# A decoder layer on one core: shorter rope tables, a fixed order at the change to the attention, and the modulation products split and moved

## The chip, the cores and the metric

The kernel runs on one core of a Trainium2 chip. The metric is the device time of one execution in microseconds (us). Before the change it is 984.95 us, the median of three runs (981.52 to 985.64).

## The reference, cut to what matters

One conditioned decoder layer, batch 1, 1024 tokens, width 1024, everything in float32:

```
shift, scale, gate = split(c @ w_ada + b_ada)          # "modulation", three times 1024
h    = rmsnorm(x, norm_gain) * (1 + scale) + shift
proj = h @ w_in       # stick-breaking q, k, v, z | latents c_q, c_kv | k_rot | mla_z | g_a, g_b
o_a  = stick_breaking_attention(q, k, v)               # 8 heads of 64
y_a  = (o_a * silu(z)) @ w_branch_a
o_b  = latent_attention(...)    # q and k from the latents; 32 of 96 dimensions turned by rope
y_b  = (o_b * silu(mla_z)) @ w_branch_b
x    = x + gate * ((sigmoid(g_a)*y_a + sigmoid(g_b)*y_b) @ w_out);   return rmsnorm(x, final_gain)
rope(x, pos): ang = pos * 10000 ** (-2i/32);  x1*cos - x2*sin, x1*sin + x2*cos
```

The cosines and sines are computed in the kernel: the angle in turns is reduced exactly in float32 pieces, and a polynomial gives the rest.

## The kernel before, in words

Large products run in float32r (a float32 that TensorE takes in one pass). To keep the precision each operand is split into a high part and a rest, and a product is three: high by high, high by rest, rest by high. A plain float32 product is used for small things only; the trace shows it as two records.

**The opening stage** (lines 419 to 685, pool `st`) makes h transposed (`hh`, `hl`: high part and rest, one tile for each of 8 blocks k of 128 channels) and, with it, the first products of `w_in`: for token half q = 0 and then 1, six accumulators (`accu[q]`: units 0 to 3 are the value projections of four token tiles in PSUM tags g, g, s, s, unit 4 is q of head pair 0 in tag s, unit 5 its k in tag o). Step n of the loop at L619 does the products of block k = n-1 for half 0, term by term (`by_term(k, 0, 0)`, `1`, `2`, six products of 512 columns each), and between them prepares block n: `turn` transposes x, `h_hi` (ScalarE) and `h_lo` (VectorE) apply the modulation. The modulation of a block (`wa` tiles of `w_ada`, loaded in four DMAs each) is summed mostly on VectorE (`mod_first`, `mod_acc`), but the parts listed in `WA_PE` go over TensorE as products with one column. `mod_sum(k)` issues all of these and then the column sums of VectorE's accumulator; `mod_out` adds the constants. `mod_sum` runs for k = 0, 1 and then for pairs of blocks at 2, 4, 6, each at step n = k.

`load`, `load_wa`, `load_x`, `load_w` issue all loads of this stage on SP's queue, in the order in which they stand. The order of the opening stage is written out: `pin_engines(first)` ties every instruction to the one before it on its engine (SP's queue among them), in the order of the program text. Everything after it is ordered by a planner that simulates the engines' times, except where `tc.issue_after(ins)` or `keep_in_program_order` says otherwise.

**The rope tables** (`rope_tables`, L139) run on VectorE during half 1. It is a generator: after each block k the loop at L673 lets it go on by nine of its `yield`s, and L684 lets it finish. It stands on VectorE's queue between the `h_lo` of the blocks 3 to 7.

**The change to the attention** (L691 on). The q and k of pair 0 are evacuated: half 0 from `qk0` in SBUF, half 1 from the accumulators; ScalarE copies the high part, VectorE makes the rest and two copies more for k. `store_v(1, t)` evacuates the values of half 1 (ScalarE high, VectorE rest, then a DMA to DRAM), and `load_v(0)` reads them back. Then come the filler jobs (`Job`, L276): each has a weight load of 512 KB (tile `raw`, two buffers, one of which is also `qk0`), a high copy on VectorE, a rest on VectorE (`le="v"`) or GpSimd (`le="p"`, the default), and two halves of 24 products (L299). Job 0 (z of pair 0) uses the PSUM tags t and o; job 1, a merge gate, uses g and g. The fillers are spread between the steps of the attention (`sb_pair`), so that TensorE always has something to do. `gate_sum` loads the weights of the residual gate in 512 KB pieces.

The lines that the change touches most:

```
        for n in range(1, KD):
            ...
            by_term(k, 0, 0)
            if PAIR_OF[n] == n:
                mod_sum(n)
                mod_out(n)
            turn(n, 0)
            by_term(k, 0, 1)
```

Of the kernel before, what the change touches and what calls it, by code (L numbers as in the profile page):

```python
# [10 lines left out]
F32 = mybir.dt.float32  # L11
# [4 lines left out]
ALU = mybir.AluOpType  # L16
# [3 lines left out]
P = 128  # L20
# [28 lines left out]
def hybrid_layer(ctx: ExitStack, tc: tile.TileContext, x, c, positions, w_ada, b_ada, norm_gain, w_in,  # L49
# [86 lines left out]
    cos_t = base.tile([P, NT, 16], F32, name="cos_t")  # L136
    sin_t = base.tile([P, NT, 16], F32, name="sin_t")

    def rope_tables(pool):  # L139
        eng = nc.vector  # L140
        n = [0]
        slots = pool.tile([P, 32, P], F32, name="rp", tag="wa", bufs=3)

        def new(keep):
            if keep is not None:
                return slots[:, keep]
            n[0] += 1
            return slots[:, n[0] % 26]

        def ts(i, s1, op0, s2=None, op1=None, keep=None):  # L150
            o = new(keep)
            eng.tensor_scalar(out=o, in0=i, scalar1=s1, scalar2=s2, op0=op0, **({"op1": op1} if op1 else {}))
            return o

        def tt(a, b, op, keep=None):
            o = new(keep)
            eng.tensor_tensor(out=o, in0=a, in1=b, op=op)
            return o

        def near(i, unit):  # L160
            m = 1.5 * 2.0 ** 23 * unit
            r = ts(i, m, ALU.add)
            return ts(r, m, ALU.subtract)

        import numpy as np
        inv = np.float32(ROPE_BASE) ** (-np.arange(0, DR, 2, dtype=np.float32) / np.float32(DR))
        ang = new(None)
        av = ang.rearrange("p (t f) -> p t f", f=16)
        for f in range(16):
            eng.tensor_scalar(out=av[:, :, f], in0=pos_c, scalar1=float(inv[f]), scalar2=None,  # L170
                              op0=ALU.mult)
            if f % 4 == 3:
                yield
        from fractions import Fraction
        pi = Fraction(31415926535897932384626433832795028841971693993751, 10 ** 49)
        total = None
        left = ang
        for e in (20, 9, -2, None):
            if e is None:
                part, k, scale = left, Fraction(1) / (2 * pi), 1.0  # L180
# [11 lines left out]
            whole = ts(part, scale, ALU.mult) if scale != 1.0 else part  # L192
            if e is None:
                fr = ts(whole, float(k), ALU.mult)
                total = tt(total, fr, ALU.add)
                break
            t1 = ts(whole, float(k1), ALU.mult)
            yield
            t1 = tt(t1, near(t1, 1.0), ALU.subtract)
            yield  # L200
            t2 = ts(whole, float(k2), ALU.mult)
            yield
            t3 = ts(whole, float(k3), ALU.mult)
            yield
            s = tt(t1, t2, ALU.add)
            yield
            s = tt(s, t3, ALU.add)
# [5 lines left out]
        q = ts(near(turn, 0.25), 4.0, ALU.mult, keep=26)  # L213
        th = ts(tt(turn, near(turn, 0.25), ALU.subtract), 2.0 * math.pi, ALU.mult, keep=27)
        yield
        t2 = tt(th, th, ALU.mult, keep=28)
        yield

        def poly(cs):
            r = ts(t2, cs[0], ALU.mult, cs[1], ALU.add)  # L220
            for cc in cs[2:]:
                r = ts(tt(r, t2, ALU.mult), cc, ALU.add)
            return r

        fact = math.factorial
        sn = tt(poly([-1.0 / fact(11), 1.0 / fact(9), -1.0 / fact(7), 1.0 / fact(5), -1.0 / fact(3)]), t2, ALU.mult)
        yield
        sn = tt(tt(sn, th, ALU.mult), th, ALU.add, keep=29)
        yield
        cs = tt(poly([1.0 / fact(12), -1.0 / fact(10), 1.0 / fact(8), -1.0 / fact(6), 1.0 / fact(4), -0.5]), t2,  # L230
                ALU.mult)
# [4 lines left out]
        yield  # L236
        m1 = tt(odd, q, ALU.mult)
        yield
        m0 = tt(ts(odd, -1.0, ALU.mult, 1.0, ALU.add), ts(q2, -0.5, ALU.mult, 1.0, ALU.add), ALU.mult)
        yield  # L240
        cv, sv = cos_t.rearrange("p t f -> p (t f)"), sin_t.rearrange("p t f -> p (t f)")
        eng.tensor_tensor(out=cv, in0=tt(m0, cs, ALU.mult), in1=tt(m1, sn, ALU.mult), op=ALU.subtract)
        eng.tensor_tensor(out=sv, in0=tt(m0, sn, ALU.mult), in1=tt(m1, cs, ALU.mult), op=ALU.add)

    def newton(r, v, n):
# [89 lines left out]
    def evac_q(m):  # L335
        st = pairs[m]

        def f(hf, ps):
            if hf == 0:
                st.q = [qk(f"q{m}a"), qk(f"q{m}b")]  # L340
            s = hsl(hf)
            for h in range(2):
# [5 lines left out]
    def evac_k(m):  # L348
        st = pairs[m]

        def f(hf, ps):
            if hf == 0:
# [3 lines left out]
            for h in range(2):  # L356
# [62 lines left out]
    with tc.tile_pool(name="start", bufs=1, **RW, side="right") as st:  # L419
# [58 lines left out]
        def scale_x(t, eng):  # L478
# [3 lines left out]
            else:  # L482
                (nc.vector if eng == "v" else nc.gpsimd).tensor_scalar(out=xts[t], in0=xts[t], scalar1=r, scalar2=None,
                                                                       op0=ALU.mult)

        def mod_first(k):
            accs[k] = st.tile([P, 2, 2 * P], F32, name="acc", tag="acc", bufs=2)[:, :, 0:width(k)]
            wa, c0 = was[k], col[:, R_C:R_C + 1]
# [5 lines left out]
        def mod_acc(k, a, b):  # L494
            for kk in range(a, b):
                if kk not in WA_PE.get(k, ()):
                    nc.vector.scalar_tensor_tensor(out=accs[k], in0=was[k][:, :, kk, :],
                                                   scalar=col[:, R_C + kk:R_C + kk + 1], in1=accs[k], op0=ALU.mult,
                                                   op1=ALU.add)

        def mod_sum(k):
            pm = pts["m"] = ps_tile("t")
            kks = WA_PE.get(k, ())
            nj = width(k) // P
            for n, (kk, j, s) in enumerate(itertools.product(kks, range(nj), range(2))):
                nc.tensor.matmul(out=pm[:, 2 * j + s:2 * j + s + 1], lhsT=was[k][:, s, kk, j * P:(j + 1) * P],
                                 rhs=col[:, R_C + kk:R_C + kk + 1], start=n == 0, stop=False)
            for j in range(nj):
                for s in range(2):
                    nc.tensor.matmul(out=pm[:, 2 * j + s:2 * j + s + 1], lhsT=accs[k][:, s, j * P:(j + 1) * P], rhs=ones_c,  # L510
                                     start=not kks, stop=not kks or (s == 1 and j == nj - 1))

        def mod_out(k0):
            pm = pts["m"]
# [26 lines left out]
        accu = {}  # L541

        def product(k, q, unit, term):
            if q not in accu:
# [50 lines left out]
        inverse(1)  # L595
        scale_x(2, "a")
        mod_acc(0, 2, 8)
        mod_sum(0)
        scale_x(3, "a")
        mod_out(0)  # L600
        nc.vector.tensor_copy(out=pos_f, in_=pos_i)
        split_w_hi(0)
        turn(0, 0)
        split_w_lo(0)
        h_hi(0, 0)
        load_w(3)
# [12 lines left out]
        for n in range(1, KD):  # L619
# [2 lines left out]
                op(i)  # L622
            by_term(k, 0, 0)
            if PAIR_OF[n] == n:
                mod_sum(n)
                mod_out(n)
            turn(n, 0)
            by_term(k, 0, 1)
            if n in (1, 2, 4):
                mod_first(2 if n == 1 else n + 2)  # L630
# [184 lines left out]

# [2 lines left out]
    def gate_sum():  # L818
# [4 lines left out]
            nc.sync.dma_start(out=wgs[k], in_=wada[:, k, 2 * D:3 * D])  # L823

        nc.gpsimd.memset(gsum, 0.0)
        nc.sync.dma_start(out=gsum[0:1], in_=b_ada[:, 2 * D:3 * D])
        load_g(0)
        load_g(1)
        yield
        for k in range(KD):  # L830
            cc = col[:, R_C + k:R_C + k + 1]
# [586 lines left out]
```

## Time and profile before

| What | us |
|---|---|
| median of three runs | 984.95 |
| the profiled execution's own time | 984.33 |
| its span, first to last instruction | 982.5 |
| TensorE busy (97% of the span) | 953.9 |
| VectorE busy (65%) | 641.5 |
| ScalarE busy (45%) | 440.3 |
| GpSimd busy (29%) | 289.8 |

All times below count from the start of the span. PE is TensorE, DVE VectorE, ACT ScalarE, POOL GpSimd, SPq the DMA queue of SP. The chain that ended last lies on PE for 92% of the span, on DVE for 4% and on DMA for 2%. "PEclk" in the table by stretches is the granted share of TensorE's 2.4 GHz; 0.50 is 1.2 GHz.

### The profile page before, as it was taken

Reading aid. Unit: us, or ns where it says so; the run is one execution under the profiler, and the core shown is the slowest. Engines: PE = TensorE matmul, PEld = TensorE weight load, DVE = VectorE, ACT = ScalarE, POOL = GpSimd, SP = SyncE. Lnnn points to the kernel's source line nnn. Section 1 sums busy time; section 2 is a strip of 40 time slices with the busy share of each in tenths; the row PEclk is TensorE's granted clock in tenths of the full one; section 3 lists DMA queues with packets and bytes.
Section 4 is the critical chain, followed back from the end, with each engine's and each line's share of the span. In section 5 each row is a group of like instructions: output and inputs, shape, how many; then the busy total and the mean of one; then the engine's idle time right before and its main releaser. Section 6 shows DMA issues by size and latency. Waiting matters only on the chain.

```text
span 982.5 us, 14349 instructions
## 1 busy us (share of the span) xinstructions
PE 953.9 (97%) x5132; PEld 824.2 (84%) x5132; DVE 641.5 (65%) x1319; ACT 440.3 (45%) x991; POOL 289.8 (29%) x256
## 2 busy tenths in 40 slices
PE   5999699999999999999999999999999999999997
PEld 4888588888888888888888999988899998878886
DVE  5657756568655966385654454864689997595654
ACT  5453324344524443444443432543488886342211
POOL 1010235344544444354453000621103441101222
PEclk9899899999999999999999999999999999999999
DMA  9911273223331141103212500579554332792232
GB/s 311 332 53 56 87 238 95 73 64 90 129 105 46 54 139 54 54 22 97 76 65 86 150 1 1 192 274 303 180 134 135 104 97 69 248 374 95 83 118 98
DMA packets 112712, 122.39 MB, mean 125 GB/s; under 512 B 14928, under 2 KB 81597, under 8 KB 112256
## 3 DMA queue, kind: packets, MB, share of 16 engines
q1 hardware_dynamic: 112550, 121.44, 39.3%
q8 instruction: 41, 0.67, 0.3%
q14 instruction: 31, 0.25, 0.1%
q10 hardware_dynamic: 90, 0.02, 0.0%
HBM read 86.80 MB, written 34.64 MB: 124 GB/s over the span
## 4 chain that ended last, share of the span: by engine, by line
PE 92%; DVE 4%; DMA 2%; issue 1%; ACT 0%; DVEq 0%; SPq 0%
PE ps_g L299 38%; PE ps_o L723 7%; PE ps_t L706 7%; PE ps_g L935 3%; PE ps_s L1354 3%; PE ps_g L1354 3%; PE ps_t L1354 3%; PE ps_s L936 3%; PE ps_s L1170 2%; PE ps_s L1172 2%; PE ps_s L551 2%; PE ps_s L1171 2%; PE ps_g L551 2%; PE ps_s L754 2%; PE ps_s L753 2%; PE ps_t L1050 2%
## 5 line engine op out<-in xcount | busy, mean ns | idle before, releaser
L299 PE MATMUL ps_g<-hh,whi 128*128 128x512 f32 x448 | 178.8, 399 | 5.4 <-DVE vo L96 5.4
L299 PE MATMUL ps_g<-hl,whi 128*128 128x512 f32 x448 | 177.7, 397 | 0.0
L299 PE MATMUL ps_g<-hh,wlo 128*128 128x512 f32 x448 | 176.8, 395 | 0.0
L757 DVE TENSOR_TENSOR_SCAN surv<-surv,diag 128x128 f32<-128x128 f32 (+3 forms) x64 | 112.6, 1764 | 41.6 <-ACT surv L755 40.8
L96 POOL TENSOR_TENSOR wlo<-raw,whi 128x1024 fp32r<-128x1024 f32 (+1 forms) x37 | 80.8, 2184 | 174.5 <-DVE whi L88 98.2
L96 DVE TENSOR_TENSOR wtl<-ps_t,wth 128x512 fp32r<-128x512 f32 (+1 forms) x192 | 101.6, 548 | 17.6 <-ACT wth L86 16.6
L761 POOL TENSOR_TENSOR beta<-beta,surv 128x127 f32<-128x127 f32 (+3 forms) x64 | 85.4, 1334 | 62.2 <-DVE surv L757 61.6
L299 PEld LDWEIGHTS ps_g<-hh,whi 128*128 128x128 f32 x448 | 85.0, 190 | 21.6 <-DVE vo L96 5.8
L86 ACT ACTIVATE wth<-ps_t 128x512 fp32r<-128x512 f32 (+1 forms) x192 | 90.0, 490 | 23.7 <-PE ps_t L706 21.0
L299 PEld LDWEIGHTS ps_g<-hh,wlo 128*128 128x128 f32 x448 | 84.9, 189 | 17.1
L299 PEld LDWEIGHTS ps_g<-hl,whi 128*128 128x128 f32 x448 | 85.0, 190 | 15.3
L391 ACT ACTIVATE ev<-ps_g 128x512 f32<-128x512 f32 x32 | 19.2, 599 | 105.4 <-PE ps_g L299 103.8
L88 DVE CAST whi<-raw 128x1024 fp32r<-128x1024 f32 (+1 forms) x38 | 24.9, 656 | 57.4 <-PE ps_g L299 43.5
L1182 ACT ACTIVATE sc<-sc,mx 128x128 f32<-128x128 f32 (+3 forms) x64 | 49.3, 771 | 15.0 <-DVE mx L1173 15.0
L1360 POOL TENSOR_TENSOR xr<-xr,fgain 128x512 f32<-128x512 f32 (+1 forms) x17 | 20.9, 1232 | 111.4 <-ACT yr L1359 107.2
L755 ACT ACTIVATE surv<-ps_s 128x512 f32<-128x512 f32 (+2 forms) x96 | 47.1, 494 | 9.0 <-PE ps_s L754 4.4
L756 ACT ACTIVATE beta<-ps_s 128x512 f32<-128x512 f32 (+2 forms) x96 | 47.7, 501 | 3.8 <-POOL beta L761 3.8
L86 ACT ACTIVATE otmp<-ps_o 64x256 f32<-64x256 f32 x64 | 24.2, 379 | 50.0 <-PE ps_o L723 48.9
L706 PE MATMUL ps_t<-ident,sc 128*128 128x128 f32 x288 | 44.9, 275 | 0.1
L706 PE MATMUL ps_t<-ident,beta 128*128 128x128 f32 x288 | 43.1, 275 | 0.0
L299 PE MATMUL ps_g<-oa,whi 128*128 128x512 f32 x128 | 41.3, 397 | 0.0
L1173 DVE CUSTOM_DVE_ANT_0 sc<-ps_s,cmask 128x512 f32<-128x512 f32 (+2 forms) x64 | 37.1, 582 | 5.8 <-PE ps_s L1172 4.4
(420 smaller groups left out, 2350.9 us busy)
## 6 DMA issues: line engine op xcount, KB each, us to landing
raw<-in_w_in SPq DMA_DIRECT2D x35, 512.0 KB, 4.0
wa<-in_w_ada SPq DMA_DIRECT2D x12, 512.0 KB, 6.0
x<-in_x SPq DMA_DIRECT2D x8, 512.0 KB, 5.4
v_d<-vo SPq DMA_DIRECT2D x8, 512.0 KB, 3.4
wg<-in_w_ada SPq DMA_DIRECT2D x8, 512.0 KB, 3.5
ga_d<-ev SPq DMA_DIRECT2D x16, 256.0 KB, 2.0
v<-v_d SPq DMA_DIRECT2D x4, 1024.0 KB
gb_d<-ev SPq DMA_DIRECT2D x16, 256.0 KB, 2.0
```

The source lines that it names most:

```text
L86: nc.scalar.activation(o, i, AF.Copy)
L96: (nc.vector if eng == "v" else nc.gpsimd).tensor_tensor(out=o, in0=full, in1=rd(hi), op=ALU.subtract)
L299: nc.tensor.matmul(out=ps, lhsT=w[:, k, :], rhs=m[k][:, hsl(hf)], start=n == 0, stop=n == last)
L551: nc.tensor.matmul(out=accu[q][unit], lhsT=m[:, tsl], rhs=w[:, 0:512], **fl)
L706: anchor[0] = nc.tensor.transpose(out=pt[:, b * P:(b + 1) * P], in_=w[:, (j0 + b) * P:(j0 + b + 1) * P], identity=ident)
L723: anchor[0] = nc.tensor.matmul(out=po[:, qs], lhsT=vtile(j), rhs=wts[j // 4][n][:, j % 4, qs], start=j == 0 and n == 0, stop=j == i and n ...
L755: nc.scalar.activation(surv[:, c0:c0 + wc], ps[:, 0:wc], AF.Sigmoid, scale=-0.125)
L756: nc.scalar.activation(beta[:, c0:c0 + wc], ps[:, 0:wc], AF.Sigmoid, scale=0.125)
L757: scan[0] = nc.vector.tensor_tensor_scan(out=surv[:, 0:w][:, ::-1], data0=surv[:, 0:w][:, ::-1], data1=diag1[:, S - w:S][:, ::-1], initial ...
L761: nc.gpsimd.tensor_tensor(out=beta[:, 0:w - 1], in0=beta[:, 0:w - 1], in1=surv[:, 1:w], op=ALU.mult)
L1182: nc.scalar.activation(sc[:, 0:w], sc[:, 0:w], AF.Exp, bias=mx[:, len(chunks) - 1:len(chunks)] if CH else mx[:, 0:1], scale=-1.0, accum_ou ...
L1354: nc.tensor.matmul(out=ps[:, 0:wc], lhsT=m[k][:, tsl], rhs=w[:, k, cs], start=k == 0 and i == 0, stop=k == KD - 1 and i == 2)
```

## The change

In five parts. (1) The rope tables: the 16 products with one frequency each become one, over a table of frequencies that GpSimd fills at the start; two steps that followed each other become one instruction with two operations, or a `scalar_tensor_tensor`. (2) `mod_sum` is split: `mod_kk(k)` holds the products of the weights, `mod_sum(k)` the column sums. `mod_kk` of 2, 4, 6 is moved up one step, to stand behind `turn` of n = 1, 3, 5. (3) `keep_warm` multiplies the identity by itself, four products into each of the accumulators named, whose content is overwritten later: twice three units before `mod_sum(0)`, one unit before the first real product. (4) The evacuations at the change to the attention get a written order, job 0 and job 1 make their rest on VectorE, and the wait of the first job half on the SP queue goes. (5) The loads of `gate_sum` are queued on SP behind `load_v(0)`.

```
+    inv_t = base.tile([P, 16], F32, name="inv_t")
+    for f in range(16):
+        nc.gpsimd.memset(inv_t[:, f:f + 1], float(inv[f]))
...
+        def stt(a, c, b, op0, op1, keep=None):
+            o = new(keep)
+            eng.scalar_tensor_tensor(out=o, in0=a, scalar=c, in1=b, op0=op0, op1=op1)
+            return o
...
-            r = ts(i, m, ALU.add)
-            return ts(r, m, ALU.subtract)
+            return ts(i, m, ALU.add, m, ALU.subtract)
...
-        for f in range(16):
-            eng.tensor_scalar(out=av[:, :, f], in0=pos_c, scalar1=float(inv[f]), scalar2=None,
-                              op0=ALU.mult)
-            if f % 4 == 3:
-                yield
+        eng.tensor_tensor(out=ang.rearrange("p (t f) -> p t f", f=16),
+                          in0=pos_c[:, :, None].broadcast_to([P, NT, 16]),
+                          in1=inv_t[:, None, :].broadcast_to([P, NT, 16]), op=ALU.mult)
+        yield
...
-            t1 = ts(whole, float(k1), ALU.mult)
+            t1 = ts(part, scale, ALU.mult, float(k1), ALU.mult)
...
-            t2 = ts(whole, float(k2), ALU.mult)
+            s = stt(part, scale * float(k2), t1, ALU.mult, ALU.add)
             yield
-            t3 = ts(whole, float(k3), ALU.mult)
-            yield
-            s = tt(t1, t2, ALU.add)
-            yield
-            s = tt(s, t3, ALU.add)
+            s = stt(part, scale * float(k3), s, ALU.mult, ALU.add)
...
-            r = ts(t2, cs[0], ALU.mult, cs[1], ALU.add)
-            for cc in cs[2:]:
-                r = ts(tt(r, t2, ALU.mult), cc, ALU.add)
+            r = ts(t2, cs[0], ALU.mult)
+            for cc in cs[1:]:
+                r = stt(r, cc, t2, ALU.add, ALU.mult)
...
+        def mod_kk(k):
+            pts["m", k] = ps_tile("t")
+            kks = WA_PE.get(k, ())
+            for n, (kk, j, s) in enumerate(itertools.product(kks, range(width(k) // P), range(2))):
+                nc.tensor.matmul(out=pts["m", k][:, 2 * j + s:2 * j + s + 1],
+                                 lhsT=was[k][:, s, kk, j * P:(j + 1) * P], rhs=col[:, R_C + kk:R_C + kk + 1],
+                                 start=n == 0, stop=False)
...
+        def keep_warm(units):
+            if 0 not in accu:
+                accu[0] = [ps_tile(t) for t in "ggssso"]
+            for u in units:
+                for j in range(4):
+                    nc.tensor.matmul(out=accu[0][u][:, j * P:(j + 1) * P], lhsT=ident, rhs=ident, start=True,
+                                     stop=True)
...
         mod_acc(0, 2, 8)
+        keep_warm(range(3))
+        mod_kk(0)
+        keep_warm(range(3))
         mod_sum(0)
...
         turn(0, 0)
+        keep_warm((4,))
...
             if PAIR_OF[n] == n:
+                if n == 1:
+                    mod_kk(n)
                 mod_sum(n)
                 mod_out(n)
             turn(n, 0)
+            if n in (1, 3, 5):
+                mod_kk(n + 1)
             by_term(k, 0, 1)
...
-    for hf in range(2):
-        evac_q(0)(hf, qk0[:, 0] if hf == 0 else accu[1][4])
-        evac_k(0)(hf, qk0[:, 1] if hf == 0 else accu[1][5])
-    for t in range(4):
-        store_v(1, t, sbp, "wt", WT_BUFS[0])
...
+    jobs[0].le = jobs[1].le = "v"
     filler = run_jobs(jobs)
-    if 1:
-        tc.keep_in_program_order(nc.scalar.activation(warm, ones_c, AF.Sigmoid))
-    with tc.issue_after(last_on("SP")), tc.issue_after(last_on("DVE")):
+    first = len(traced)
+    jobs[0].prep()
+    evac_q(0)(0, qk0[:, 0])
+    evac_k(0)(0, qk0[:, 1])
+    jobs[1].prep()
+    for t in range(4):
+        store_v(1, t, sbp, "wt", WT_BUFS[0])
+    for h in range(2):
+        evac_q(0)(1, accu[1][4], (h,))
+        evac_k(0)(1, accu[1][5], (h,))
+        if h == 0:
+            nc.scalar.activation(warm, ones_c, AF.Sigmoid)
+    load_v(0)
+    pin_engines(first)
+    with tc.issue_after(last_on("ACT")), tc.issue_after(last_on("DVE")):
         advance(filler, 1)
     advance(filler, 1)
-    load_v(0)
...
+        with tc.issue_after(last_on("SP")):
+            nc.sync.dma_start(out=gsum[0:1], in_=b_ada[:, 2 * D:3 * D])
+            load_g(0)
+            load_g(1)
```

## Rows read from the trace of the kernel before

**Rows 1.** PE's waits in the whole span: total us, times, longest.
```profile
PE ps_t L122 <- DMA vec<-in_norm_gain: 5.9, 1, 5.9
PE ps_g L299 <- DVE vo L96: 5.4, 1, 5.4
PE ps_t L506 <- DMA wa<-in_w_ada: 3.5, 2, 3.2
```

**Rows 2.** PE in order of time: the wait in the last block.
```profile
106.10 0.50 PE L554 MATMUL ps_o<-hl,w3h 128*128 128x512 f32 x1 [2.26 <-DVE hl L96]
```

**Rows 3.** Stretches: us, busy of each engine (instructions), PEclk, DMA share, GB/s.
```profile
17.10:25.20 8.10, 8.07 (x27) 7.11 (x28) 5.87 (x12) 3.77 (x6) 0.00 (x0) 1.00 1.09 348
32.10:35.40 3.30, 3.30 (x9) 2.60 (x8) 2.59 (x4) 1.63 (x3) 0.00 (x0) 0.50 1.04 382
45.70:49.00 3.30, 3.30 (x9) 2.63 (x8) 3.09 (x11) 1.55 (x4) 0.60 (x1) 0.50 0.47 164
107.20:110.50 3.30, 3.30 (x9) 2.57 (x8) 0.78 (x1) 1.67 (x3) 0.00 (x0) 0.50 0.39 86
120.80:127.50 6.70, 5.00 (x12) 3.95 (x13) 6.42 (x12) 1.23 (x3) 0.00 (x0) 0.50 0.64 253
127.70:980.00 852.30, 845.96 (x4642) 734.96 (x4640) 558.38 (x1094) 384.87 (x904) 276.44 (x243) 1.00 0.38 117
```

**Rows 4.** The chain that ended last, opening: start, us, what, records merged.
```profile
14.29 1.01 PE ps_t L510 x4
15.31 0.97 PE ps_t L527 x4
17.13 1.22 PE ps_g L551 x2
...
23.37 0.85 PE ps_g L551 x2
...
28.44 1.68 PE ps_t L506 x16
30.12 0.89 PE ps_t L510 x8
31.02 0.50 PE ps_t L527 x4
...
33.55 0.85 PE ps_g L551 x2
...
35.86 0.47 PE ps_g L551 x2
```

**Rows 5.** DVE by line, 79.9 to 105.3: count, busy us, mean ns, idle before.
```profile
L157 DVE TENSOR_TENSOR rp<-rp 128x128 f32<-128x128 f32 x36 | 10.3, 290 | 0.9
L152 DVE TENSOR_SCALAR rp<-rp 128x128 f32<-128x128 f32 x46 | 9.9, 225 | 1.0
L170 DVE TENSOR_SCALAR rp<-pos_c 128x8 f32<-128x8 f32 x16 | 1.3, 168 | 0.0
```

**Rows 6.** Tile wa, VectorE's sums: ns min/median/max, first and last start, forms.
```profile
L497 DVE SCALAR_TENSOR_TENSOR acc<-wa,col,acc x24: 480/744/753, 11.0 to 54.8; 128x512 f32<-128x512 f32 x15, 128x256 f32<-128x256 f32 x9
```

**Rows 7.** DVE in order of time, at the change to the attention.
```profile
105.36 0.68 DVE L96 TENSOR_TENSOR hl<-ht,hh 128x512 fp32r<-128x512 f32 x1
...
106.75 1.23 DVE L96 TENSOR_TENSOR wlo<-raw,whi 128x1024 fp32r<-128x1024 f32 x1
113.37 0.69 DVE L88 CAST whi<-raw 128x1024 fp32r<-128x1024 f32 x1 [5.39 <-DMA raw<-in_w_in]
...
114.81 2.77 DVE L96 TENSOR_TENSOR q0b<-qk,q0b 64x512 fp32r<-64x512 f32 x1
```

**Rows 8.** ACT in order of time: last ht of half 1.
```profile
97.13 0.77 ACT L535 ACTIVATE ht<-ps_t,ab 128x512 f32<-128x512 f32 x1
```

**Rows 9.** The chain that ended last: job 1's first half.
```profile
122.50 8.09 PE ps_g L299 x24
```

**Rows 10.** ACT in order of time, opening: the wait for the third `wa`.
```profile
20.94 0.72 ACT L492 ACTIVATE acc<-wa,col 128x512 f32<-128x512 f32 x1 [2.12 <-DMA wa<-in_w_ada]
```

More of the change, by code (lines that the diff above doesn't have):

```diff
@@ L137, in hybrid_layer @@
     sin_t = base.tile([P, NT, 16], F32, name="sin_t")
+    import numpy as np
+    inv = np.float32(ROPE_BASE) ** (-np.arange(0, DR, 2, dtype=np.float32) / np.float32(DR))
+    inv_t = base.tile([P, 16], F32, name="inv_t")
+    for f in range(16):
+        nc.gpsimd.memset(inv_t[:, f:f + 1], float(inv[f]))
     def rope_tables(pool):
@@ L191, in rope_tables @@
             k3 = k - k1 - k2
-            whole = ts(part, scale, ALU.mult) if scale != 1.0 else part
             if e is None:
-                fr = ts(whole, float(k), ALU.mult)
-                total = tt(total, fr, ALU.add)
+                total = stt(part, float(k), total, ALU.mult, ALU.add)
                 break
-            t1 = ts(whole, float(k1), ALU.mult)
+            t1 = ts(part, scale, ALU.mult, float(k1), ALU.mult)
             yield
@@ L212, in rope_tables @@
         yield
-        q = ts(near(turn, 0.25), 4.0, ALU.mult, keep=26)
-        th = ts(tt(turn, near(turn, 0.25), ALU.subtract), 2.0 * math.pi, ALU.mult, keep=27)
+        quarter = near(turn, 0.25)
+        q = ts(quarter, 4.0, ALU.mult, keep=26)
+        yield
+        th = ts(tt(turn, quarter, ALU.subtract), 2.0 * math.pi, ALU.mult, keep=27)
         yield
@@ L217, in rope_tables, with poly_t2 @@
         yield
-        def poly(cs):
-            r = ts(t2, cs[0], ALU.mult, cs[1], ALU.add)
-            for cc in cs[2:]:
-                r = ts(tt(r, t2, ALU.mult), cc, ALU.add)
+        def poly_t2(cs):
+            r = ts(t2, cs[0], ALU.mult)
+            for cc in cs[1:]:
+                r = stt(r, cc, t2, ALU.add, ALU.mult)
             return r
         fact = math.factorial
-        sn = tt(poly([-1.0 / fact(11), 1.0 / fact(9), -1.0 / fact(7), 1.0 / fact(5), -1.0 / fact(3)]), t2, ALU.mult)
+        sn = poly_t2([-1.0 / fact(11), 1.0 / fact(9), -1.0 / fact(7), 1.0 / fact(5), -1.0 / fact(3)])
         yield
@@ L229, in rope_tables @@
         yield
-        cs = tt(poly([1.0 / fact(12), -1.0 / fact(10), 1.0 / fact(8), -1.0 / fact(6), 1.0 / fact(4), -0.5]), t2,
-                ALU.mult)
+        cs = poly_t2([1.0 / fact(12), -1.0 / fact(10), 1.0 / fact(8), -1.0 / fact(6), 1.0 / fact(4), -0.5])
+        yield
         cs = ts(cs, 1.0, ALU.add)
@@ L235, in rope_tables @@
         odd = ts(q2, 1.0, ALU.is_equal)
-        yield
         m1 = tt(odd, q, ALU.mult)
         yield
-        m0 = tt(ts(odd, -1.0, ALU.mult, 1.0, ALU.add), ts(q2, -0.5, ALU.mult, 1.0, ALU.add), ALU.mult)
+        m0 = stt(odd, 1.0, ts(q2, 0.5, ALU.mult, 1.0, ALU.subtract), ALU.subtract, ALU.mult)
         yield
@@ L242, in rope_tables @@
         eng.tensor_tensor(out=cv, in0=tt(m0, cs, ALU.mult), in1=tt(m1, sn, ALU.mult), op=ALU.subtract)
+        yield
         eng.tensor_tensor(out=sv, in0=tt(m0, sn, ALU.mult), in1=tt(m1, cs, ALU.mult), op=ALU.add)
@@ L336, in evac_q, with f @@
         st = pairs[m]
-        def f(hf, ps):
-            if hf == 0:
+        def f(hf, ps, heads=(0, 1)):
+            if hf == 0 and 0 in heads:
                 st.q = [qk(f"q{m}a"), qk(f"q{m}b")]
             s = hsl(hf)
-            for h in range(2):
+            for h in heads:
                 r0, r1 = (slice(0, 64), slice(64, 128)) if h == 0 else (slice(64, 128), slice(0, 64))
@@ L349, in evac_k, with f @@
         st = pairs[m]
-        def f(hf, ps):
-            if hf == 0:
+        def f(hf, ps, heads=(0, 1)):
+            if hf == 0 and 0 in heads:
                 st.k = [qk(f"k{m}a"), qk(f"k{m}b")]
@@ L355, in f @@
             s = hsl(hf)
-            for h in range(2):
+            for h in heads:
                 r0, r1 = (slice(0, 64), slice(64, 128)) if h == 0 else (slice(64, 128), slice(0, 64))
@@ L484, in scale_x @@
                                                                        op0=ALU.mult)
+        accu = {}
         def mod_first(k):
@@ L499, in mod_acc @@
                                                    op1=ALU.add)
+        def mod_kk(k):
[5 more added lines that the diff above has]
+                                 start=n == 0, stop=False)
         def mod_sum(k):
-            pm = pts["m"] = ps_tile("t")
-            kks = WA_PE.get(k, ())
             nj = width(k) // P
[L505 to L511, printed above, removed]
+            for j, s in itertools.product(range(nj), range(2)):
+                nc.tensor.matmul(out=pts["m", k][:, 2 * j + s:2 * j + s + 1], lhsT=accs[k][:, s, j * P:(j + 1) * P],
+                                 rhs=ones_c, start=False, stop=s == 1 and j == nj - 1)
+        def keep_warm(units):
[5 more added lines that the diff above has]
+                                     stop=True)
         def mod_out(k0):
-            pm = pts["m"]
+            pm = pts["m", k0]
             for j in range(width(k0) // P):
@@ L539, in h_lo @@
             rest("v", hl[k][:, hs], hts[k, q][:, a * P:b * P], hh[k][:, hs])
-        accu = {}
         def product(k, q, unit, term):
@@ L825, in gate_sum @@
         nc.gpsimd.memset(gsum, 0.0)
-        nc.sync.dma_start(out=gsum[0:1], in_=b_ada[:, 2 * D:3 * D])
-        load_g(0)
-        load_g(1)
+        with tc.issue_after(last_on("SP")):
+            nc.sync.dma_start(out=gsum[0:1], in_=b_ada[:, 2 * D:3 * D])
+            load_g(0)
+            load_g(1)
         yield
```

3 lines of the change are left out of this document (removed).

## The prediction

> **What bounds the kernel now.** I read PE's waits first [rows 1], then the stretches by granted clock [rows 3], then the chain and the engines where these point. From 127.7 to 980 PE is busy 846.0 of 852.3 us at full clock [rows 3]: what shifts PE's work there earlier shifts the end by as much. Everything to be had lies before. PE waits there for the first load (5.9), for a modulation weight (3.2), for `vo` (5.4) [rows 1] and for `hl` (2.3) [rows 2]. And four stretches ran at 1.2 GHz after PE had idled or done only tiny products [rows 3]. A pair of 512-column products takes 0.47 us at the high clock (at 35.86) and 0.85 at the low one (at 33.55) [rows 4]: 0.233 against 0.427 each, so each product done at low costs 0.19. The pair at 23.37 took 0.85 too, though the stretch around it prints PEclk 1.00 [rows 3, 4]: that 1.00 stands ahead of the first change the trace recorded, and by the pace PE ran at 1.2 GHz there as well. The same stretch shows the DMA engines full (share 1.09, 348 GB/s).
>
> The sum is made against the profiled execution: span 982.5, time 984.3, 0.6 below the median of the runs.
>
> **Part 1, rope tables.** Counted in the code, 100 VectorE operations become 57: 22 two-tensor, 18 with a scalar, 17 `scalar_tensor_tensor`. The rows show 98 of the 100: 10.3 + 9.9 + 1.3 us, 21.5 in all [rows 5] (two more write the tables). After: 22 x 0.29 + 18 x 0.225 + 17 of the new kind. That kind is shown only at twice the size and more, 0.48 to 0.75 [rows 6]; bounds 0.22 and 0.48, I take 0.35, since a two-tensor operation of this size takes 0.29 and the new one's shortest at 256 is 0.48. Sum 16.4 us, 5 less (3 to 7). On DVE this alone is worth nothing; what counts is what stands behind it. The last `hl` ran at 105.36 [rows 7] although its input was there at 97.13 + 0.77 = 97.9 [rows 8]: 34 rope operations stood ahead of it in the fixed order, because all the rest of the table came out in one `advance`. Counting the new `yield`s (14, 15, 24 operations after k = 1, 2, 3, then 3), 24 stand between the `hl` of blocks 5 and 6 and three ahead of the last, block 7's. That one then runs at 97.9 to 98.6, PE asks for it at 106.10 - 2.26 = 103.8 [rows 2], and the wait goes.
>
> **Part 2, the change to the attention.** PE waited 5.4 us for `vo` [rows 1]. Behind it: DVE stood 5.39 us for job 1's load at 113.37 with all the evacuations queued behind that cast, and then spent 2.77 us on one 64-row rest, where `hl`, with twice the rows, takes 0.68, while (by the code) GpSimd made job 1's rest [rows 7]. The new order puts the evacuations of half 0 ahead of that cast, and the rest on DVE (+1.23).
>
> In before's time and with 0.69 for every evacuation, DVE afterwards: last `hl` to 98.6, job 0's cast 0.69 and rest 1.23 to 100.5, eight operations of half 0 to 106.0, job 1's cast and rest to 108.0, four `vo` to 110.7, half 1's eight to 116.2. Job 1's load can start at 100.5 if it takes job 0's buffer, and took 5.4 us beside the two gate loads, which now stand behind `load_v(0)`: 105.9, no wait. If it takes `qk0`'s buffer it starts at 106 and DVE waits to 111.4; everything behind is 5.4 later.
>
> PE afterwards: the product that waited is the third of 18 in the last block, so the block starts at about 103.2 and ends, without the stall, at 107.4; job 0's first half (24 x 0.233 = 5.6) ends at 113.0; job 1's first half needs the first `vo` (108.7, or 114.1 with the other buffer) and ends at 118.6, where before it ended at 122.50 + 8.09 = 130.6 [rows 9]. So 12.0 are to be had: 2.3 + 5.4 of waits, and 3.9 from the two low stretches behind them (8 products from 107.2, 12 from 122.5, at 0.19 each). I take off 0.8 for small new waits: 11.2, bounds 5 and 12. What is late next is job 0's second half, which needs the bank of the last k evacuation (115 to 120): the cover is job 1's first half, if the planner puts it ahead, as it did before.
>
> What the edit adds elsewhere: 16 GpSimd memsets at the start, while that engine waits for x, and gate loads that come later but are used over the whole attention: nothing.
>
> **Part 3, the opening.** An identity product is not in the trace of before. It would show as two records: `mod_sum(0)`, at 14.29, is two products and four records [rows 4]. Nearest by shape is the 128x128 transpose: four in 0.97 at low, 0.50 at high [rows 4]. Bounds per record: below, a one-column record (16 in 1.68: 0.105 at high); above, a 512-column product (0.233 and 0.427). I take the transposes' 0.24 and 0.125. The first 12 products (24 records) start at 6.2 and stand in PE's wait for `wa`; at low they end at 12.0. `mod_kk(0)` (12 records) then takes 1.3 at high, the second 12 products 3.0: `mod_sum(0)` starts at 16.3 instead of 14.29, 2.0 late. At high it and `turn` take 0.95, ScalarE 0.8; the last four products cover that (8 x 0.125 = 1.0). First real product 18.2 (before 17.13), six of them done at 19.6.
>
> Then `mod_kk(1)` 0.85, a wait for VectorE's accumulator (about 21.1), `mod_sum(1)` and `turn` 0.95: 22.0. And here stands what was moved: `mod_kk(2)`, 16 records, ahead of `by_term(0, 0, 1)`. It needs all four loads of its `wa`. The first half was in at 20.94, where ScalarE had waited for it [rows 10]; the second, 1.05 MB more through a full 348 GB/s [rows 3], is in about 3.0 later, at 23.9, whatever PE does. So PE waits about a microsecond, in front of products that need nothing of it, and `by_term(0, 0, 1)` starts at about 25.0 instead of 23.37. By then PE has done 5 us of one-column products, transposes and waiting, more than the 3.1 us of it at 28.44 that came before the fall at 32.10 (of three such blocks, two were followed by a fall) [rows 3, 4]; I expect one low stretch (1.6) here. From there to `by_term(2, 0, 0)`: 30 products 7.0, `mod_sum(2)` 0.9, `turn` 0.5, the low stretch 1.6: 35.0, against 35.86. Gain 0.8; with two low stretches -0.8, with none 2.5.
>
> Later steps: `mod_kk(4)` and `mod_kk(6)` find their weights loaded, and the products of 1.68 and 0.89 + 0.50 [rows 4] no longer stand in one block of 3.1 us. So the fall at 45.70 should not come: 1.6 (0 to 1.6). Opening: 2.4.
>
> A page of the Trainium skill speaks against the identity products: "TensorE: Matmul & The Clock Gate", Part 4: PE-mode transpose, says a transpose does not count as PE being busy, so the clock doesn't rise on it. Transposes and one-column products indeed did not hold the clock here: after 3.1 us of them it fell. Plain products with the identity it does not name, and no row shows them; if they are to the clock what transposes are, the third rival's sum holds.
>
> **Sum.** 11.2 + 2.4 = 13.6; 984.3 - 13.6 = 970.7, or 971.3 against the median.
>
> **The rivals.**
> 1. *The opening gains fully*: no low stretch at 25 (1.7) and no new wait at the change (0.8), the weights a little sooner: 968.5. For it: from 127.7 on, with no long pause, PE kept the high clock to 980 [rows 3]. Against it: `mod_kk(2)`'s wait for a full DMA queue.
> 2. *A wait takes the place of the one removed*: job 1's load takes `qk0`'s buffer, or the planner puts job 0's second half next on PE. PE then waits at 113 for the k bank: 2 to 5 us and a low stretch (1.6): 4 to 6 less, 976. For it: the order on PE is not written out. Against it: the planner chose job 1 before.
> 3. *The identity products don't raise the clock.* Then 24 records take 5.8, `mod_kk(0)` 3.0, the second group 5.8: `mod_sum(0)` at 20.8, the first product 6.5 late (23.6). Of that about 1.5 comes back, since `mod_kk(2)`'s weights are then there. Opening -5 + 1.6 instead of 2.4: 977.
> 4. *Slower*: the identity products cost as much as 512-column ones, at low (0.427 a record). Then the two groups end at 16.4 and 29.7, `mod_sum(0)` starts 15 us late, the last four products add 2.6 behind the transposes, and some 2 come back: -16 + 1.6 + 11.2 is 3 slower: 988. It outweighs the change from about 0.37 a record. For it: no row shows such a product. Against it: a transpose of the same shape takes 0.24.
> 5. *The fixed order changes nothing at the change to the attention*, since the evacuations can't start before something I don't see (memory of the first stage that must come free). Then the 5.4 and the 2.3 of its low stretch stay: 979.
>
> **How the numbers follow.** Forecast 60% (own range 969 to 974), rival 1 10%, 2 12%, 3 9%, 4 3%, 5 6%. The range 967 to 979 takes in the first four and leaves out rival 4, half of 5 and the outer ends, among them that the planner orders the attention otherwise once its start moves (1 to 3 us either way). About 0.5% (4.9 us) is what a measurement of this kernel can tell from no change: faster is below 980.0. Rival 4 and some of 5 lie outside, and with something unforeseen I give faster 0.88, same 0.08, slower 0.04.
>
> **What would show it.** In the changed profile: 57 rope operations in about 16 us and the last `hl` before 100; no PE wait for `vo` or `hl`, no half clock between 90 and 125; job 1's products about 14 us earlier; identity products at about 0.24, then 0.125 a record; `by_term(0, 0, 1)` at about 25 behind a wait for `wa`, and a low stretch there; none near 45. Wrong would be: the first real product after 20, a PE wait of over 2 us near 113, or PE idle after 130 by more than before.

## The result, and the profile after

The changed kernel takes 970.88 us (median of four runs, 969.66 to 971.1) against 985.3 for the kernel before on the same chip (981.52 to 985.82): a ratio of 0.9861 [0.9843, 0.9879]. The forecast was 971.3. The profiled execution took 970.71 us, its span is 968.9.

The time came from where the forecast looked for it, the change to the attention. PE's longest waits, as in [rows 1]:

```profile
PE ps_t L122 <- DMA vec<-in_norm_gain: 6.1, 1, 6.1
PE ps_g L301 <- ACT whi L86: 1.1, 1, 1.1
PE ps_t L516 <- DVE acc L501: 1.0, 1, 1.0
...
PE ps_t L509 <- DMA wa<-in_w_ada: 0.2, 1, 0.2
```

The waits for `vo` (5.4) and `hl` (2.3) are gone. Stretches of the changed kernel, columns as in [rows 3]:

```profile
11.30:21.60 10.30, 9.19 (x74) 8.60 (x73) 8.32 (x23) 5.42 (x7) 1.96 (x1) 1.00 1.10 321
21.60:31.80 10.20, 9.99 (x35) 8.60 (x35) 5.90 (x10) 3.50 (x5) 0.00 (x0) 0.50 1.09 349
...
106.30:111.70 5.40, 5.40 (x25) 4.46 (x24) 5.28 (x10) 5.09 (x9) 0.00 (x0) 1.00 0.85 260
111.70:117.70 6.00, 6.00 (x31) 5.02 (x30) 2.22 (x5) 0.94 (x4) 0.00 (x0) 1.00 0.57 230
117.70:967.00 849.30, 841.83 (x4626) 731.24 (x4624) 556.44 (x1090) 385.24 (x903) 277.04 (x243) 1.00 0.38 118
```

Three of the low stretches of [rows 3] are gone, those near 46, 107 and 121 us. In place of the fourth, at 32.1, one of 10.2 us stands in the opening, from 21.6 to 31.8. VectorE at the change to the attention, in order of time, beside [rows 7]: nothing in it waits for a load, and the 64-row rest takes 0.69 us instead of 2.77.

```profile
97.21 0.69 DVE L96 TENSOR_TENSOR hl<-ht,hh 128x512 fp32r<-128x512 f32 x1
...
98.60 1.23 DVE L96 TENSOR_TENSOR wlo<-raw,whi 128x1024 fp32r<-128x1024 f32 x1
...
100.58 0.69 DVE L96 TENSOR_TENSOR q0b<-qk,q0b 64x512 fp32r<-64x512 f32 x1
...
104.32 0.69 DVE L88 CAST whi<-raw 128x1024 fp32r<-128x1024 f32 x1
...
106.26 1.37 DVE L96 TENSOR_TENSOR vo<-ps_g,vo 128x512 fp32r<-128x512 f32 x2
```

Job 1's first product on PE stands at 111.77 instead of 122.50, with no wait ahead of it:

```profile
111.77 0.39 PE L301 MATMUL ps_g<-hh,whi 128*128 128x512 f32 x1
...
117.45 0.40 PE L301 MATMUL ps_g<-hh,wlo 128*128 128x512 f32 x1
```

The second row is the last product of job 1's first half: the half ends at 117.85, where it ended at 130.59 before [rows 9]. Behind that PE's waits of 0.2 us and more sum up to 2.5 us, against 2.1 before, so the lead at job 1 is carried to the end: the span is 13.6 shorter.

### The profile page after: what moved, and what is told of

Its sections match the earlier page's. It is cut to its first block, busy times and chain, and to the rows that moved or that the text cites. A ratio compares the mean times of both kernels' runs of the same rounds, so it can differ in the third digit from the quotient of the medians.

```text
span 968.9 us, 14443 instructions
## 1 busy us (share of the span) xinstructions
PE 952.0 (98%) x5188; PEld 825.5 (85%) x5188; DVE 633.1 (65%) x1277; ACT 440.9 (45%) x991; POOL 288.0 (30%) x271
## 4 chain that ended last, share of the span: by engine, by line
PE 92%; DMA 6%; DVE 1%; SPq 1%; issue 0%; ACT 0%; POOL 0%; DVEq 0%; POOLq 0%
PE ps_g L301 36%; PE ps_o L738 7%; PE ps_t L721 7%; PE ps_g L963 3%; PE ps_g L1382 3%; PE ps_s L1382 3%; PE ps_t L1382 3%; PE ps_s L964 3%; PE ps_g L564 2%; PE ps_s L564 2%; DMA wa<-in_w_ada 2%; PE ps_s L1198 2%; PE ps_s L1199 2%; PE ps_s L1200 2%; PE ps_s L769 2%; PE ps_s L768 2%
## 5 line engine op out<-in xcount | busy, mean ns | idle before, releaser
L772 DVE TENSOR_TENSOR_SCAN surv<-surv,diag 128x128 f32<-128x128 f32 (+3 forms) x64 | 109.6, 1717 | 48.5 <-ACT surv L770 47.4
L96 POOL TENSOR_TENSOR wlo<-raw,whi 128x1024 fp32r<-128x1024 f32 (+1 forms) x36 | 78.0, 2166 | 113.6 <-DVE whi L88 35.9
L775 POOL MEMSET beta<- 128x1 f32 x64 | 6.4, 100 | 128.5 <-ACT beta L771 125.5
L750 POOL TENSOR_TENSOR oga<-oga,zs 64x256 f32<-64x256 f32 x32 | 36.0, 1126 | 19.6 <-DVE oga L748 18.4
```

What stands on the lines that cost most here:

```text
L96: (nc.vector if eng == "v" else nc.gpsimd).tensor_tensor(out=o, in0=full, in1=rd(hi), op=ALU.subtract)
L772: scan[0] = nc.vector.tensor_tensor_scan(out=surv[:, 0:w][:, ::-1], data0=surv[:, 0:w][:, ::-1], data1=diag1[:, S - w:S][:, ::-1], initial ...
```

## The experiments

Differences in us below are (1 - ratio) x 985. The ratio is that of each version to the kernel before on the same chip, and stands with its 95% interval. First the two halves of the change at the attention, then the opening, then a better version.

**e5: the rope tables alone** (before, with part 1 and nothing else):

```
...
-            r = ts(t2, cs[0], ALU.mult, cs[1], ALU.add)
-            for cc in cs[2:]:
-                r = ts(tt(r, t2, ALU.mult), cc, ALU.add)
+            r = ts(t2, cs[0], ALU.mult)
+            for cc in cs[1:]:
+                r = stt(r, cc, t2, ALU.add, ALU.mult)
...
```

> Only the shorter rope tables; opening and the change to the attention as before. Theory (all that stands behind the tables on VectorE comes earlier): the wait for hl and its low stretch go (3.9 us), and job 1's load, its cast and the evacuations behind it start some 7 us earlier while PE arrives 4 us earlier, so the wait for vo shrinks too, from 5.4 to 1 to 3: 5 to 8 us faster, 976 to 979. Rival (only the hl wait goes, and PE waits for vo the longer): the gain is given back, under 2 us.

Measured: 971.45 us, 0.9866 [0.985, 0.9883], 13.2 faster, where 5 to 8 were expected. One part alone brings what the whole change brings. VectorE in e5, in order of time:

```profile
97.38 0.69 DVE L96 TENSOR_TENSOR hl<-ht,hh 128x512 fp32r<-128x512 f32 x1
97.99 0.69 DVE L88 CAST whi<-raw 128x1024 fp32r<-128x1024 f32 x1
98.78 1.23 DVE L96 TENSOR_TENSOR wlo<-raw,whi 128x1024 fp32r<-128x1024 f32 x1
104.19 0.69 DVE L88 CAST whi<-raw 128x1024 fp32r<-128x1024 f32 x1 [4.19 <-DMA raw<-in_w_in]
...
105.63 2.78 DVE L96 TENSOR_TENSOR q0b<-qk,q0b 64x512 fp32r<-64x512 f32 x1
...
112.58 1.29 DVE L96 TENSOR_TENSOR vo<-ps_g,vo 128x512 fp32r<-128x512 f32 x2
```

The wait for job 1's load and the slow rest, which the prediction put behind the `vo` wait, are both still there. Only the whole row of operations stands 8.0 us earlier (`hl` at 97.38 instead of 105.36), and from job 1's cast on 9.2 (104.19 instead of 113.37). When the load is issued, in the kernel before and in e5 (tile `raw`: min, median and max ns, first and last issue):

```profile
L272 SPq DMA_DIRECT2D raw<-in_w_in x2: 379/382/384, 108.0 to 117.1; - x2
```

```profile
L274 SPq DMA_DIRECT2D raw<-in_w_in x3: 378/383/1062, 100.0 to 116.4; - x3
```

In both it goes out the moment VectorE has finished job 0's `wlo` (106.75 + 1.23 = 107.98 in [rows 7]; 98.78 + 1.23 = 100.01 in e5). So in the trace a chain leads from the tables to PE: tables, `hl`, job 0's cast and rest, job 1's load, its cast, the evacuations, `vo`, and job 1's first product. PE's wait for `vo` is 1.2 us in e5:

```profile
PE ps_g L301 <- DVE vo L96: 1.2, 1, 1.2
```

In e5's trace PE runs at the high clock from 102 to 119 (granted 1.00). So 10.4 us of the gain can be named: 2.3 + 1.6 for the `hl` wait and the low stretch behind it, 5.4 - 1.2 + 2.3 for the `vo` wait and its low stretch.

**e6: the written order alone** (before, with parts 4 and 5 and the long tables):

```
...
+    jobs[0].le = jobs[1].le = "v"
...
+    jobs[0].prep()
+    evac_q(0)(0, qk0[:, 0])
+    evac_k(0)(0, qk0[:, 1])
+    jobs[1].prep()
...
+    pin_engines(first)
...
```

> Only the written order at the change to the attention (with the rest of jobs 0 and 1 on VectorE and the gate loads queued behind); rope tables and opening as before. Theory: the wait for hl and its low stretch stay, the wait for vo (5.4) and its low stretch (2.3) go: 6.5 to 8 us faster, 976 to 977.5. Rival (the order needs VectorE free at 98): VectorE is late by the 7 us of the longer tables, vo comes after PE's 24 products of job 0, and a wait of 2 us or more for vo stays: under 5 us faster.

Measured: 976.27 us, 0.9911 [0.9894, 0.9928], 8.8 faster, with the median in the range that was expected. The `vo` wait goes, and PE's wait for `hl` stays. The low stretch behind it, however, did not come in this trace (second fence, columns as in [rows 3]: granted 1.00 from 100 to 125):

```profile
107.27 0.50 PE L565 MATMUL ps_o<-hl,w3h 128*128 128x512 f32 x1 [2.25 <-DVE hl L96]
```

```profile
100.00:125.00 25.00, 22.75 (x102) 18.46 (x101) 22.95 (x53) 9.41 (x19) 1.41 (x4) 1.00 0.49 157
```

So the wait of 2.3 us was followed by a fall of the clock in the kernel before and not in e6. Either part alone takes away most or all of the `vo` wait: the tables leave 1.2 of 5.4 by making VectorE early, and the order leaves nothing by putting fewer steps between job 1's cast and `vo` (in e6 they start at 113.68 and 115.62, in the kernel before at 113.37 and 121.7). 13.2 and 8.8 are therefore not to be added.

**e2: both at the change to the attention, without the new opening** (the changed kernel with all `mod_kk` back in `mod_sum`'s place and no `keep_warm`):

```
-        keep_warm(range(3))
...
-                if n == 1:
-                    mod_kk(n)
+                mod_kk(n)
...
-            if n in (1, 3, 5):
-                mod_kk(n + 1)
```

> Parts 1, 2, 4 and 5 alone: no identity products, and all products of mod_kk back at mod_sum, so the opening is in before's order. Theory: the change to the attention is worth 11 to 12.5 us alone: 973 to 974. Rival: it gains more than its own stalls (over 13 us, under 972), the opening then costing time in the changed kernel; or under 10, and the two parts need each other.

Measured: 972.0 us, 0.9889 [0.9869, 0.9909], 10.9 faster. That is no more than e5, and 11 to 12.5 lie within its interval (9.0 to 12.9).

**e13: the last `hl` ahead of the tables' rest** (before, its long tables unchanged in number):

```
-                advance(rope, 9)
+                if k != 4:
+                    advance(rope, 9)
```

> The kernel before with its long tables; nine operations of the tables are left out of the turn at the fifth k block and come later, so that the last hl stands ahead of them on VectorE. VectorE's sum of work is unchanged. Theory: the wait for hl (2.3 us) and the low clock behind it (1.6) go, but VectorE is as late as before at job 1's whi, so the wait there grows by nearly as much: 0 to 1.5 us faster, 982.5 to 984.5. Rival, the prediction's own pricing of the tables: the hl wait and its low clock go for good, 4 us faster, 980 to 981.

Measured: 978.56 us, 0.9946 [0.9928, 0.9964], 5.3 faster: the theory's 0 to 1.5 failed, and the rival's 4 is nearer. It does not isolate the place of `hl` as meant: with the tables ending later, the planner also put pair 0's evacuations and first scores ahead of job 1. VectorE in e13:

```profile
97.97 0.69 DVE L96 TENSOR_TENSOR hl<-ht,hh 128x512 fp32r<-128x512 f32 x1 [1.74 <-ACT ht L535]
...
107.83 0.68 DVE L88 CAST whi<-raw 128x1024 fp32r<-128x1024 f32 x1
...
110.59 0.69 DVE L96 TENSOR_TENSOR q0b<-qk,q0b 64x512 fp32r<-64x512 f32 x1
...
114.24 1.29 DVE L96 TENSOR_TENSOR vo<-ps_g,vo 128x512 fp32r<-128x512 f32 x2
...
118.96 0.69 DVE L88 CAST whi<-raw 128x1024 fp32r<-128x1024 f32 x1
```

It shows that the lead can be had in part without a single operation less, by what stands ahead of what. How much of it is `hl`'s place and how much the planner's other order stays open.

**e1: the opening alone** (before, with parts 2 and 3):

```
...
+        keep_warm(range(3))
+        mod_kk(0)
+        keep_warm(range(3))
...
+            if n in (1, 3, 5):
+                mod_kk(n + 1)
...
```

> Only part 3: the kernel before with the identity products and the split and moved modulation products; rope tables and the change to the attention as before. Theory: the opening's gain is lost in mod_kk(2)'s wait for the third wa in front of by_term(0,0,1), so 0 to 1.5 us faster than before (984 to 985), with by_term(0,0,1) at about 26 and a long low stretch around it. Rival (the sum on record): 2.4 us faster, 982.9. If it is over 3 us faster, the opening is worth more than the trace after shows.

Measured: 981.52 us, 0.9988 [0.9974, 1.0002]: 1.2 faster, as expected, but not clear of the noise. In its trace `by_term(0, 0, 1)` starts at 26.09, and PE runs low from 21.6 to 31.8, as in the changed kernel.

**e4: the changed kernel without the identity products** (the three `keep_warm` lines out).

> The changed kernel without the identity products. Theory: TensorE then runs at 1.2 GHz from the first product to about 25, but it has to wait for the third wa (24.7) anyway, so the products lose at most 1.5 us: 970 to 972.5. Rival (the identity products carry the opening's gain): over 2.5 us slower than the changed kernel, 973.5 or more.

Measured: 970.19 us, 0.9869 [0.9846, 0.9893]: the same as the changed kernel, as expected. PE in the opening, in order of time, first the changed kernel, then e4:

```profile
6.29 3.78 PE L524 MATMUL ps_g<-ident 128*128 128x128 f32 x16
...
14.82 1.06 PE L524 MATMUL ps_s<-ident 128*128 128x128 f32 x8
15.71 0.50 PE L516 MATMUL ps_t<-ones_c,acc 128*128 128x1 f32 x4
...
17.59 0.72 PE L564 MATMUL ps_g<-w3h,hh 128*128 128x512 f32 x2
...
22.38 2.15 PE L509 MATMUL ps_t<-col,wa 128*128 128x1 f32 x10
24.73 1.44 PE L509 MATMUL ps_t<-col,wa 128*128 128x1 f32 x6 [0.21 <-DMA wa<-in_w_ada]
26.03 1.20 PE L564 MATMUL ps_g<-w3l,hh 128*128 128x512 f32 x2
...
36.95 0.62 PE L564 MATMUL ps_g<-w3h,hh 128*128 128x512 f32 x2
```

```profile
17.14 1.22 PE L564 MATMUL ps_g<-w3h,hh 128*128 128x512 f32 x2 [0.87 <-ACT hh L549]
...
23.17 3.41 PE L509 MATMUL ps_t<-col,wa 128*128 128x1 f32 x16
26.44 1.20 PE L564 MATMUL ps_g<-w3l,hh 128*128 128x512 f32 x2
```

The identity products do bring the first products up to the high clock (a pair in 0.72 instead of 1.22). But six products later both kernels come to the modulation's small products, the last of them `mod_kk(2)`, and leave them within about 0.4 us of each other (26.03 and 26.44).

**e3: `mod_kk(2)` back at `mod_sum(2)`**, and **e9: that without the identity products.**

```
-                if n == 1:
+                if n in (1, 2):
                     mod_kk(n)
...
-            if n in (1, 3, 5):
+            if n in (3, 5):
```

> The changed kernel with mod_kk(2) alone put back to stand right ahead of mod_sum(2); mod_kk(4) and mod_kk(6) stay moved. Theory: by_term(0,0,1) starts at about 22.5 instead of 26, mod_kk(2) finds its weights there, the low stretch is shorter: 2 to 3.5 us faster than the changed kernel (967.5 to 969). Rival (the wait only moves to the next need of the same weights, VectorE's sum for mod_sum(2)): within 0.7 us of the changed kernel, 970 to 971.5.

> The changed kernel with mod_kk(2) put back to mod_sum(2) and without the identity products. Theory: with the wait for the weights gone, the clock at the first products counts: by_term(0,0,1) starts at 23.4 as before instead of 22.5 to 23.7, at 1.2 GHz until 25: 0.5 to 2 us slower than e3 (968.4 to 970). Rival (the identity products are worth nothing in any place): equal to e3 within 0.4 us, 967.5 to 968.3.

Measured: e3 967.9 us, 0.9851 [0.983, 0.9871]; e9 968.13, 0.9838 [0.9822, 0.9855]. By the medians both lie some 3 us below the changed kernel, as expected of e3; by the ratios the intervals of e3 and the changed kernel overlap, so the size is not settled. e3 and e9 are equal, which was the rival of e9: the identity products buy nothing here either.

**e10: the rest term first** (e3, with `by_term(0, 0, 1)` ahead of all of block 1's modulation):

```
+            if n == 1:
+                by_term(k, 0, 1)
             if PAIR_OF[n] == n:
...
-            by_term(k, 0, 1)
+            if n > 1:
+                by_term(k, 0, 1)
```

> e3 (mod_kk(2) back), and at n = 1 the six products by_term(0,0,1) moved ahead of mod_kk(1), mod_sum(1) and turn(1): they need nothing of these, and fill TensorE's wait of about 1 us for VectorE's accumulator. Theory: 1 to 2.5 us faster than e3 (965.5 to 967). Rival (the delay only moves to h of block 1, which the next products need): equal to e3.

Measured: 966.38 us, 0.9815 [0.9802, 0.9829], 18.2 faster than before, outside the changed kernel's interval, and 1.5 below e3 by the medians, as expected. Of all the versions its median is the lowest but for e11. The products that need nothing of `wa` now fill the time in which PE waited for VectorE's accumulator:

```profile
18.54 0.62 PE L564 MATMUL ps_g<-w3l,hh 128*128 128x512 f32 x2
...
32.15 0.73 PE L564 MATMUL ps_g<-w3h,hh 128*128 128x512 f32 x2
```

Here the first row is `by_term(0, 0, 1)` (26.03 in the changed kernel), the second `by_term(2, 0, 0)` (36.95).

The changed kernel was measured a second time beside e11, e12 and e13 (**after_again**): 970.41 us, 0.9856 [0.9837, 0.9875], as expected.

> The changed kernel as it is, beside the three others of this group, so that they can be set against it on the same chip. Both theories: 969.5 to 971.5 us, 13 to 14 below the kernel before.

**e11: e10 without the identity products** (the three `keep_warm` lines out).

> e10 (mod_kk(2) back in its place, by_term(0,0,1) ahead of pair 1's weight transposes) without the identity products. Theory: in e10 the first products stand earlier, so a TensorE that comes to them at the low level pays now: the first 12 products of the opening run at half speed until about 25 us, 1 to 2.5 us slower than e10, 967.4 to 969. Rival: as in e3 against e9, the opening waits for its loads anyway and the identity products buy nothing: equal to e10 within 0.5 us.

Measured: 966.27 us, 0.9819 [0.9799, 0.9839], equal to e10: the rival. Its first products run low (a pair in 1.22), but from 21.6 on its clock stays high to 960, while e10's falls once, from 26.9 to 30.3:

```profile
21.60:960.00 938.40, 933.28 (x5103) 808.73 (x5101) 620.65 (x1241) 429.12 (x973) 283.37 (x247) 1.00 0.39 123
```

```profile
26.90:30.30 3.40, 3.40 (x14) 3.01 (x14) 0.94 (x5) 0.00 (x0) 0.00 (x0) 0.50 1.09 348
```

The other pairs show the same. The traces of the changed kernel, e3 and e10 show the clock fall after the identity products had raised it (at 21.6, 23.6 and 26.9), while those of e4, e9 and e11, without them, come to the high clock later, by the pace of their products, and record no fall after that. What the identity products win in pace is largely given back there, and in e3's trace the clock fell once among them already (16 records took 3.50 us there), and the first real product came later (19.30, against 17.17 in e9).

**e12: e10 with the planner's order at the change to the attention**, and the gate's loads where they were:

```
...
-    jobs[0].le = jobs[1].le = "v"
...
-    pin_engines(first)
-    with tc.issue_after(last_on("ACT")), tc.issue_after(last_on("DVE")):
+    with tc.issue_after(last_on("SP")), tc.issue_after(last_on("DVE")):
...
```

> e10 with the planner's own order at the change to the attention, and the gate's loads where the kernel before has them; the shorter tables stay. Theory: behind shorter tables the written order has little left to bring, at most 1.5 us: 966.4 to 968.5. Rival: the written order is worth several us of its own there: 969 or more.

Measured: 967.51 us, 0.9829 [0.9809, 0.9849]. Against e10 that is 1.4 us slower by the ratios and 1.1 by the medians, with intervals that overlap: of the 8.8 us that the written order is worth with the long tables, some 1 us is left behind the short ones, and it is not clear of the noise. PE waits 1.0 us for `vo` in e12.

## Why the prediction was right, and where it was not

**The total.** The forecast was 13.6 less on the span, and 13.6 was measured. That the two agree to a tenth is luck. The opening was to bring 2.4 and had brought 1.0 when PE came to the last block (first product of the block, before and after):

```profile
103.21 0.39 PE L554 MATMUL ps_o<-hh,w3h 128*128 128x512 f32 x1
```

```profile
102.25 0.39 PE L567 MATMUL ps_o<-hh,w3h 128*128 128x512 f32 x1
```

At the end of job 1's first half the lead was 12.7 (117.85 instead of 130.59), so the change to the attention brought 11.8, where 11.2 was forecast. The last 0.9 came behind it: 0.46 of it are four small products of the first scores, which stand ahead of that end only in the changed kernel, and the rest stays open.

**Part 1, the tables.** The 57 operations took 15.2 us, not 16.4:

```profile
L163 DVE TENSOR_TENSOR rp<-rp 128x128 f32<-128x128 f32 x19 | 5.3, 290 | 0.5
L168 DVE SCALAR_TENSOR_TENSOR rp<-rp 128x128 f32<-128x128 f32 x17 | 5.0, 292 | 0.5
L158 DVE TENSOR_SCALAR rp<-rp 128x128 f32<-128x128 f32 x18 | 4.0, 225 | 0.4
```

To these come 0.9 for the three of the angle and the two results. The new kind costs 0.292 us, what the two-tensor kind costs, where 0.35 was taken from double-sized rows. The saving was 6.9 us, where 5 was forecast: the 21.5 us before that the prediction set against its 16.4 lacked the two writes of the tables, 0.6 us. (Its counts of 14, 15, 24 and 3 operations also make 56; the third is 25 in the trace.) `hl` ran at 97.21 and its wait went, as forecast. The step that failed is the price behind the sentence that "on DVE this alone is worth nothing; what counts is what stands behind it": only the `hl` wait and the low clock after it were counted there (2.3 + 1.6 = 3.9 us). VectorE's lateness went on from `hl` through job 0's rest into job 1's load. [Rows 7] already held the link: VectorE's wait of 5.39 us began at 113.37 - 5.39 = 107.98, the end of job 0's `wlo`. e5 shows what the tables are worth alone: 13.2.

**Part 2, the order.** Its mechanism was right: the load of job 1 took job 0's buffer, VectorE did not wait, and job 1's half ended at 117.85 (forecast 118.6). The 12.0 that the prediction had "to be had" is the difference of its two end times; the terms it names, 2.3 + 5.4 + 3.9, make 11.6. The 5.4 was credited to the order alone; e5 and e6 show that either part removes most or all of it. The 0.8 taken off for new waits was not needed: no wait came in the place of the old one.

**Part 3, the opening.** The identity records took 0.22 to 0.24 us low (16 in 3.78, 8 in 1.75) and 0.13 high, against 0.24 and 0.125. By that pace they raised the clock, which was high from about 11.4 on, so the third and fourth rivals fell. Of the Trainium skill's page "TensorE: Matmul & The Clock Gate", Part 4: PE-mode transpose, the rule that transposes do not count as busy does not reach plain products with the identity: this trace shows them raising the clock. The mis-sized term is what `mod_kk(2)` costs ahead of ready products: `wa` came at 24.7 (forecast 23.9), `by_term(0, 0, 1)` started at 26.03 (25.0), and PE ran low for 10.2 us instead of one stretch of 3.3. The fall came at 21.6, ahead of `mod_kk(2)` and not behind it. With `mod_kk(2)` back in its place (e3) the clock fell too, at 23.6, but for 3.4 us only. `by_term(2, 0, 0)` came 1.25 later than before (36.95 against this row of the kernel before), not 0.8 earlier:

```profile
35.70 0.63 PE L551 MATMUL ps_g<-w3h,hh 128*128 128x512 f32 x2
```

In a second execution of the changed kernel (after_again) the low clock lasted 6.8 us there, so this term moves from one execution to the next. The fall near 46 did not come, as forecast, and that gave back 1.6. The other traces bear this out: each of the four others whose opening is in before's order (e2, e5, e6, e13) has a low stretch between 45 and 60, and none whose `mod_kk(4)` and `mod_kk(6)` are moved has one there. That the identity products were worth having was wrong in three pairs (e4, e9 and e11 against the kernels with them).

**Rivals.** The first (the opening gains fully) fell with the low stretch from 21.6 on. The second (a wait for the k bank) and the fifth (nothing changes at the attention) are excluded by the waits above. Of the signs, job 1's products came 10.7 us (the first) to 12.7 us (the last) earlier, not 14.

## What to carry to other kernels

When one engine runs late in a fixed order, follow its lateness through everything that it releases, loads into reused buffers included: two waits with different names can be one lateness, and then a remedy where it starts takes most of both away, while a remedy further down takes only the second. Credit for a wait belongs to what its chain starts from, and only each part alone shows it. Ahead of ready products put nothing that still needs a load, and before filling a wait with work that warms the clock, ask whether the next wait takes the lead back.

## What the runs showed of the hardware

A `scalar_tensor_tensor` of 128x128 in float32 on VectorE costs what a `tensor_tensor` of that size does (0.292 against 0.290 us), so joining two steps saves a whole operation.

The rest `q0b`, two SBUF inputs on VectorE, took 2.77 to 2.78 us in the kernel before, e5 and e12, where GpSimd made job 1's rest at the same moment, and 0.69 in the changed kernel, e6 and e13, where it did not. GpSimd in e5, in order of time:

```profile
105.02 2.84 POOL L96 TENSOR_TENSOR wlo<-raw,whi 128x1024 fp32r<-128x1024 f32 x1 [52.72 <-DVE whi L88]
```

It ended at 107.86, and `q0b` at 105.63 + 2.78 = 108.41. That is 0.55 later, about the time that an undisturbed one takes. The Trainium skill, "SBUF — State Buffer", section "Who interferes with whom", says that a VectorE instruction with two SBUF inputs contends with a GpSimd instruction that reads SBUF. The same page of the Trainium skill, section "Summary: rules for kernel authors", says that the second one to issue then blocks fully until the first has finished. The traces agree with both.
